# First groups of five sub-layers: hi products of six k first, squares on VectorE, statistics one piece later

## The chip, the cores and the metric

The kernel runs on one core of one Trainium2 chip. The metric is the device time of one launch in microseconds. TensorE is called PE here, VectorE DVE, ScalarE ACT, GpSimd POOL, SyncE SP.

## The reference

One step of a hybrid streaming encoder with two layers, in float32, for a prompt of 16 + 256 frames and a running stream of 32. Each layer has three sub-layers, each wrapped in two RMS norms:

```python
def rmsnorm(x, g):
    x32 = x.astype(jnp.float32)
    y = x32 * lax.rsqrt(jnp.mean(x32 * x32, axis=-1, keepdims=True) + EPS)
    return y.astype(x.dtype) * g

def half_ffn(x, g_pre, w_in, w_out, g_post):
    gate, up = jnp.split(rmsnorm(x, g_pre) @ w_in, 2, axis=-1)
    return x + 0.5 * rmsnorm((jax.nn.silu(gate) * up) @ w_out, g_post)
...
    for l in range(DEPTH):
        xp = half_ffn(xp, norm_ffn1_pre[l], ffn1_w_in[l], ffn1_w_out[l], norm_ffn1_post[l])
        ...
        mp, k_p, v_p, s_p = mixer_prompt(rmsnorm(xp, norm_mix_pre[l]), w_in[l], attn_sinks[l], key_valid)
        xp = xp + rmsnorm(mp @ w_out[l], norm_mix_post[l])
        ...
        xp = half_ffn(xp, norm_ffn2_pre[l], ffn2_w_in[l], ffn2_w_out[l], norm_ffn2_post[l])
```

The model width is 1024, the inner width of an FFN 2816. The mixer projects to 2816 columns, runs sliding-window attention and retention on them, and projects back.

## The kernel before, in words

**Layout.** Features lie on the 128 partitions, the 304 tokens (16 + 256 + 32) on the free axis. `x` is eight blocks (k = 0 to 7) of 128 x 304. The last FFN works on 288 tokens.

**Products.** An f32 product is made of three fp32r matmuls (`mm3`): weight hi by activation hi (L257), weight lo by activation hi (L258), weight hi by activation lo (L260). A *piece* is a 128 x 512 block of weights as hi and lo. `group4` fills four PSUM banks from eight pieces, one per k, so 12 matmuls per piece and 96 per group; its last two pieces (`tail`) go bank by bank. `group2` is the mixer's form with two banks and four pieces.

**Weights.** SP loads raw weights (four buffers ahead), ACT copies a piece to hi (L205), DVE subtracts to lo (L208). `advance` issues splits while buffers allow and while their number is under `st["cap"]`; it is called from `tick`, which a virtual clock drives. `tick` also runs the entries of the list `later` that are due. So the order of every engine's instructions is fixed when the program is written. For the first group of a sub-layer 8 (FFN 1 and mixer) or 4 (second FFN) pieces have buffers of their own (`xhi`, `xlo`).

**A seam.** Five sub-layers follow another one: 1 the mixer of layer 0, 2 its second FFN, 3 the first FFN of layer 1, 4 its mixer, 5 its second FFN. At a seam `pre_norm` makes the eight hi activations (`act_hi`, ACT) and lo activations (`act_lo`, DVE) from `x`, which the last sub-layer's result has to be added to (`step`, DVE, after POOL's multiplications by `s`, L546), and the sum of the squares of `x` (`stat_sq`: ACT squares, POOL or DVE adds). The factor 1/rms of a token is left out of the products and multiplied in behind them. `stats` makes it: a matmul with ones sums `acc` over the partitions (L483, f32, two passes), then DVE, ACT (a root) and DVE (`reciprocal`) give `rb`. In an FFN `pair(0, 0)` and `pair(0, 1)` then take the four banks of the first group to `hh` and `hl` (DVE `tg`, ACT `sg`, DVE `tu`, ACT `hh`, DVE `hl`); in the mixer `done_kv` and `done_q` take them.

**The first group of a seam, before.** `lead=2`: the hi products (L257, L258) of k = 0 and 1 go first, 16 matmuls, then their lo products (L260, 8 matmuls), then k = 2 and on with all three. `act_lo(k)` stands on DVE between the steps of `x`. Of the seven additions of squares four are on POOL (k up to `KA`), three on DVE. `stats` stands in the middle of the tail, its matmul in a bank of its own; its end lifts `st["cap"]`, which until then allows 11 pieces from the sub-layer's start. `hl` lies in memory that the mixer's `kr`, `qr` and other tiles had used, so at seams 2 and 5 its first writer waits for the mixer's last work on them (`state_out`: ACT copies `kr`, L835, POOL multiplies, L838 to L841, SP moves four pieces, POOL adds, L845).

Of the kernel before, what the change touches and what calls it, by code (L numbers as in the profile page):

```python
# [11 lines left out]
ACTF = mybir.ActivationFunctionType  # L12
# [4 lines left out]
DM = 1024  # L17
# [25 lines left out]
HOLD = 12  # L43
X2 = 1000
TAILF = 4
CAP0 = 14
SQ0 = 500
SQD = 500
PREP = 800
KA = 6  # L50
START = (11000, 11713)
D_UNIT = 4100
D_NORM = 2800
# [12 lines left out]
UNSCALE = 1500  # L66
EXTRA = (8, 4)
RAWS = 4


def shape_tables():
# [35 lines left out]
def tile_hybrid_step(ctx, tc, I, O):  # L107
# [9 lines left out]
    def bank():  # L117
        return ps.tile([P, 512], F32, tag="bk", name="bk")
# [320 lines left out]
    def pre_norm(pre, prev):  # L439

        ua = acts(2 * KD)
        acc = small("acc")
        rb = small("rb")
        if prev:
            lo0 = prev.first(ua)
            for k in range(1, KD + 1):
                if k < KD:
                    prev.step(k)
                    act_hi(k, ua, pre)
                if k == 1:  # L450
                    lo0()
                if k > 2:
                    act_lo(k - 1, ua, pre)
                if k < 2:
                    act_lo(k, ua, pre)
                if k > 1:
                    stat_sq(k - 1, acc, 1, DVE if k > KA else POOL)
            prev.residual0()
            stat_sq(0, acc, 1, DVE)
        else:  # L460
            for k in range(4):
                act_hi(k, ua, pre)
                split_one()
                act_lo(k, ua, pre)

            def rest():
                x_in(1)
                start.close()

            def prep(k):  # L470
                act_hi(k, ua, pre)
                act_lo(k, ua, pre)
            later.append((X2, rest))
            for k in range(4, KD):
                later.append((X2 + PREP * (k - 3), lambda k=k: prep(k)))
            for k in range(KD):
                later.append((X2 + SQ0 + SQD * k, lambda k=k: stat_sq(k, acc, 0)))
            later.sort(key=lambda e: e[0])
        st["cap"] = st["use"] + (11 if prev else CAP0)

        def stats():
            b = bank()
            PE.matmul(out=b[:, T0:N], lhsT=ones, rhs=acc[:, T0:], start=True, stop=True)  # L483
            sd = small("sd")
            if prev is None:
                ACT.activation(out=sd[:, T0:], in_=b[:, T0:N], func=ACTF.Sqrt, scale=1.0 / DM, bias=epst)
            else:
                DVE.scalar_tensor_tensor(out=sd[:, T0:], in0=b[:, T0:N], scalar=1.0 / DM, in1=prev.se[:, T0:], op0=ALU.mult,
                                         op1=ALU.add)
                ACT.activation(out=sd[:, T0:], in_=sd[:, T0:], func=ACTF.Sqrt)  # L490
            DVE.reciprocal(out=rb[:, T0:], in_=sd[:, T0:])
            st["cap"] = 1 << 30

        return (lambda k: ua[k][:, T0:]), (lambda k: ua[KD + k][:, T0:]), rb, stats
# [4 lines left out]
    class Post:  # L499
# [41 lines left out]
        def first(self, ua):  # L541
            t, y = self.xg[:, T0:], self.bk[0][:, :N - T0]
            gg = gprod[:, 2 * (self.post[0] // 2) + self.post[1]:][:, 0:1]
            DVE.tensor_tensor(out=t, in0=self.sp, in1=t, op=ALU.mult)
            for j in range(1, KD):
                POOL.tensor_tensor(out=x[:, j, T0:], in0=x[:, j, T0:], in1=self.s[:, T0:], op=ALU.mult)  # L546
            DVE.scalar_tensor_tensor(out=ua[0][:, T0:], in0=y, scalar=gg, in1=t, op0=ALU.mult, op1=ALU.add)

            def lo():
                DVE.scalar_tensor_tensor(out=t, in0=y, scalar=gg, in1=t, op0=ALU.mult, op1=ALU.add)  # L550
                DVE.tensor_tensor(out=ua[KD][:, T0:], in0=t, in1=ua[0][:, T0:].bitcast(F32), op=ALU.subtract)
            return lo

        def residual0(self):
            DVE.tensor_tensor(out=x[:, 0, T0:], in0=x[:, 0, T0:], in1=self.s[:, T0:], op=ALU.mult)
# [24 lines left out]
    def ffn(pre, post, nxt, prev, after=None):  # L580
# [5 lines left out]
        with tc.tile_pool(name="ffn", bufs=1, reuse_waits="tile") as fp, ExitStack() as late:  # L586
# [14 lines left out]
            def done(g):  # L601
                def f(m, bk):
                    if g and m >= 2:
                        pair(g, m - 2, bk)
                    if g == 0 and m == 1 and prev:
                        stats()
                return f

            for g in range(KF // 2):
                if g == 1:  # L610
# [3 lines left out]
                        fin.start(late.enter_context(tc.tile_pool(name="late", bufs=1, reuse_waits="tile")))  # L614
                    if not prev:
                        stats()
                    for j in range(2):
                        pair(0, j, bk)
                if g == 2 and prev and last:
                    prev.inverse()  # L620
                    prev.unscale()
# [3 lines left out]
                    late_gains()  # L625
                if last and 4 <= g < 10:
                    fin.x_in(*divmod(g - 4, 2))
                bk = group4(KD, xh, xl, n, (0, 2, 1, 3), done(g), lead=2 if prev and g == 0 else 1)
            if prev and not last:
                later.append((clock[0] + UNSCALE, prev.inverse))  # L630
                later.append((clock[0] + 2 * UNSCALE, prev.unscale))
# [104 lines left out]
    def mixer(l, prev):  # L736
# [418 lines left out]
                    DVE.tensor_tensor(out=ml[2 + p][:, T0:], in0=zo[p - 2][1], in1=mh[2 + p][:, T0:].bitcast(F32),  # L1155
                                      op=ALU.subtract)

        first = group4(KD, xh, xl, N, (2, 3, 0, 1), lambda m, bk: stats() if m == 0 else None, lead=2)
        close_extra()
        done_kv(0, first[2:])  # L1160
        done_kv(1, first[2:])
        ACT.preload_act_table(ACTF.Exp)
        advance(2)
        for m in range(2):
            done_q(0)(m, first)
        rot_tables()
        xq = [lambda k, f=f: f(k)[:, t0:] for f in (xh, xl)]
        group2(*xq, N - t0, done_q(1))
        for i in range(2):
# [63 lines left out]
```

## Time and profile before

| what | value |
|---|---|
| median of 3 runs | 1207.5 us (1207.25 to 1207.78) |
| profiled execution | 1207.33 us, of which span 1205.5 us |
| mean granted clock of PE | 0.996 |
| PE busy | 1179.0 us, 98% of the span, 8716 instructions |
| DVE, ACT, POOL busy | 833.0, 592.2, 187.1 us |
| first matmul of seams 1 to 5 at | 237.84, 378.67, 606.35, 833.13, 970.19 us |

Busy time is the time in which an engine executes instructions of the profile. PE is the engine that is nearly always busy, so what counts at a seam is how long PE takes from its first matmul to a later one, beside the number of matmuls between. The granted clock is the share of full speed at which the throttle let PE run.

### The profile page before, as it was taken

To read this page: it belongs to the slowest core of one execution; us is meant where nothing else is said; L and a number is where in the kernel's file an instruction comes from. 1 tells how busy PE (TensorE), PEld (TensorE's weight loads), DVE (VectorE), ACT (ScalarE), POOL (GpSimd) and SP (SyncE) were. 2 spreads that over 40 slices of the span, in tenths; PEclk is the share of its full clock that TensorE was granted. 3 is DMA by queue.
4 is the path that set the end of the run, shared out by engine and by line. 5 is a ranking of instruction groups with operands and counts; after the bars stand their busy time and mean duration, and the time that the engine had idled before them with its cause. 6 is when DMAs were issued, how large, how long until landed. Compare 5 with 4: busy or idle time off the path is not lost. (4 is left out here: it accounts for less than half of the span.)

```text
span 1205.5 us, 22774 instructions
## 1 busy us (share of the span) xinstructions
PE 1179.0 (98%) x8716; PEld 1146.9 (95%) x8716; DVE 833.0 (69%) x1497; ACT 592.2 (49%) x1211; POOL 187.1 (16%) x199
## 2 busy tenths in 40 slices
PE   9999999999999999999999999999999999999995
PEld 8999999998899999999989999999988999999995
DVE  7766664587888766675586665747778888766543
ACT  6644444455455545444454444445554655554442
POOL 4200001130143200022030000313101353000000
PEclk9999999999999999999999999999999999999998
DMA  7655455633425554555616445556434436655531
GB/s 229 173 169 178 142 177 159 205 121 109 125 73 156 160 173 141 166 164 159 207 57 192 141 149 177 175 161 199 127 91 133 123 97 199 195 151 179 179 105 40
DMA packets 155309, 182.51 MB, mean 151 GB/s; under 512 B 12016, under 2 KB 125984, under 8 KB 154944
## 3 DMA queue, kind: packets, MB, share of 16 engines
q1 hardware_dynamic: 153488, 178.84, 48.4%
q0 software_dynamic: 1344, 1.76, 0.7%
q8 instruction: 68, 1.11, 0.4%
q10 hardware_dynamic: 368, 0.47, 0.1%
q14 instruction: 41, 0.34, 0.1%
HBM read 175.70 MB, written 2.23 MB: 148 GB/s over the span
## 5 line engine op out<-in xcount | busy, mean ns | idle before, releaser
L257 PE MATMUL bk<-act,hi 128*128 128x304 f32 (+1 forms) x1696 | 515.4, 306 | 1.3 <-ACT hi L205 1.0
L208 DVE TENSOR_TENSOR lo<-raw,hi 128x512 fp32r<-128x512 f32 x616 | 420.9, 729 | 127.2 <-ACT hi L205 123.8
L258 PE MATMUL bk<-act,lo 128*128 128x304 f32 (+1 forms) x1696 | 505.4, 300 | 0.7 <-DVE lo L208 0.7
L260 PE MATMUL bk<-act,hi 128*128 128x304 f32 (+1 forms) x1696 | 489.8, 301 | 2.6 <-DVE act L427 1.2
L205 ACT ACTIVATE hi<-raw 128x512 fp32r<-128x512 f32 x615 | 351.3, 622 | 138.0 <-PE bk L260 111.0
L257 PEld LDWEIGHTS bk<-act,hi 128*128 128x128 f32 x1696 | 319.1, 188 | 7.4 <-issue 3.2
L258 PEld LDWEIGHTS bk<-act,lo 128*128 128x128 f32 x1696 | 319.1, 188 | 2.0 <-DVE lo L208 1.3
L260 PEld LDWEIGHTS bk<-act,hi 128*128 128x128 f32 x1696 | 312.8, 188 | 4.2 <-DVE act L1155 2.4
L257 PE MATMUL bk<-hh,hi 128*128 128x304 f32 (+1 forms) x704 | 210.7, 300 | 0.0
L258 PE MATMUL bk<-hh,lo 128*128 128x304 f32 (+1 forms) x704 | 210.2, 299 | 0.0
L260 PE MATMUL bk<-hl,hi 128*128 128x304 f32 (+1 forms) x704 | 207.8, 301 | 0.0
L595 ACT ACTIVATE sg<-tg 128x304 f32<-128x304 f32 (+1 forms) x88 | 40.0, 455 | 196.5 <-DVE tg L594 196.5
L257 PEld LDWEIGHTS bk<-hh,hi 128*128 128x128 f32 x704 | 132.5, 188 | 0.0
L258 PEld LDWEIGHTS bk<-hh,lo 128*128 128x128 f32 x704 | 132.3, 188 | 0.0
L260 PEld LDWEIGHTS bk<-hl,hi 128*128 128x128 f32 x704 | 131.0, 188 | 0.0
L594 DVE TENSOR_TENSOR tg<-bk,rb 128x304 f32<-128x304 f32 (+1 forms) x88 | 41.0, 466 | 85.9 <-PE bk L260 85.8
L574 POOL TENSOR_TENSOR x<-x,rs 128x304 f32<-128x304 f32 (+1 forms) x40 | 45.4, 1168 | 291.5 <-DVE rs L570 291.5
L599 DVE TENSOR_TENSOR hl<-tu,hh 128x304 fp32r<-128x304 f32 (+1 forms) x88 | 41.5, 472 | 47.6 <-ACT hh L598 45.0
L598 ACT ACTIVATE hh<-tu 128x304 fp32r<-128x304 f32 (+1 forms) x88 | 40.0, 455 | 59.4 <-DVE tu L597 59.4
L513 POOL TENSOR_TENSOR acc<-acc,sq 128x304 f32<-128x304 f32 (+1 forms) x12 | 10.1, 838 | 322.1 <-ACT sq L510 321.5
L546 POOL TENSOR_TENSOR x<-x,s 128x304 f32<-128x304 f32 (+1 forms) x35 | 31.3, 931 | 141.7 <-ACT s L538 141.7
L597 DVE TENSOR_TENSOR tu<-tu,sg 128x304 f32<-128x304 f32 (+1 forms) x88 | 41.8, 475 | 14.2 <-ACT sg L595 9.6
(240 smaller groups left out, 1077.8 us busy)
## 6 DMA issues: line engine op xcount, KB each, us to landing
raw<-in_ffn_w_in_dram SPq DMA_DIRECT2D x352, 256.0 KB, 4.7
raw<-in_ffn_w_out_dram SPq DMA_DIRECT2D x88, 512.0 KB, 4.6
raw<-in_w_in_dram SPq DMA_DIRECT2D x36, 512.0 KB, 4.2
raw<-in_w_out_dram SPq DMA_DIRECT2D x16, 512.0 KB, 3.9
raw<-in_w_in_dram SPq DMA_DIRECT2D x16, 256.0 KB, 3.0
dec<-in_dec_dram SPq DMA_DIRECT2D x2, 1280.0 KB, 7.0
t<-t SPq DMA_DIRECT2D x24, 76.0 KB, 2.1
out_dram<-xgm SPq DMA_DIRECT2D x2, 384.0 KB, 3.6
```

The lines of the kernel that those rows point to most:

```text
L205: ACT.activation(out=hi, in_=r, func=ACTF.Copy)
L208: DVE.tensor_tensor(out=lo, in0=r, in1=hi.bitcast(F32), op=ALU.subtract)
L257: PE.matmul(out=out, lhsT=a, rhs=xh, start=first, stop=False)
L258: PE.matmul(out=out, lhsT=b, rhs=xh, start=False, stop=False)
L260: PE.matmul(out=out, lhsT=a, rhs=xl, start=False, stop=last)
L546: POOL.tensor_tensor(out=x[:, j, T0:], in0=x[:, j, T0:], in1=self.s[:, T0:], op=ALU.mult)
L574: POOL.tensor_tensor(out=x[:, k, T0:], in0=x[:, k, T0:], in1=self.rs[:, T0:], op=ALU.mult)
L594: DVE.tensor_tensor(out=tg[:, T0:], in0=bk[j][:, :n], in1=rb[:, T0:], op=ALU.mult)
L595: ACT.activation(out=sg[:, T0:], in_=tg[:, T0:], func=ACTF.Silu)
L597: DVE.tensor_tensor(out=tu[:, T0:], in0=tu[:, T0:], in1=sg[:, T0:], op=ALU.mult)
L598: ACT.activation(out=hh[a][:, T0:], in_=tu[:, T0:], func=ACTF.Copy)
L599: DVE.tensor_tensor(out=hl[a][:, T0:], in0=tu[:, T0:], in1=hh[a][:, T0:].bitcast(F32), op=ALU.subtract)
```

## The change

In the first group of each of the five seams the hi products of k = 0 to 5 come first (`LEAD = 6`, 48 matmuls), then their lo products (24), then k = 6 and 7. All `act_lo` stand on DVE behind all steps of `x`, and all seven additions of squares stand behind those, on DVE. `first` gives the two instructions of the lo activation of k = 0 apart, behind steps 2 and 3. `stats` runs behind the first piece of the second group (in the mixer behind the first half of one), as an entry of `later`, with what uses `rb` in the same entry; its matmul is two of half the tokens, into free columns of the first group's own banks 0 and 1. The cap on splits is 13 pieces where it was 11. The mixer's `advance(2)` between `done_kv` and `done_q` is gone. The first sub-layer of the program, which follows none, is as it was.

```diff
@@ -43,11 +43,11 @@
 HOLD = 12
 X2 = 1000
 TAILF = 4
+CAP = 13
 CAP0 = 14
 SQ0 = 500
 SQD = 500
 PREP = 800
-KA = 6
 START = (11000, 11713)
 D_UNIT = 4100
 D_NORM = 2800
@@ -66,6 +66,8 @@
 UNSCALE = 1500
 EXTRA = (8, 4)
 RAWS = 4
+LEAD = 6
+STATS = 1500
 
 
 def shape_tables():
@@ -442,19 +444,16 @@
         acc = small("acc")
         rb = small("rb")
         if prev:
-            lo0 = prev.first(ua)
-            for k in range(1, KD + 1):
-                if k < KD:
-                    prev.step(k)
-                    act_hi(k, ua, pre)
-                if k == 1:
-                    lo0()
-                if k > 2:
-                    act_lo(k - 1, ua, pre)
-                if k < 2:
-                    act_lo(k, ua, pre)
-                if k > 1:
-                    stat_sq(k - 1, acc, 1, DVE if k > KA else POOL)
+            low = prev.first(ua)
+            for k in range(1, KD):
+                prev.step(k)
+                act_hi(k, ua, pre)
+                if k in (2, 3):
+                    low[k - 2]()
+            for k in range(1, KD):
+                act_lo(k, ua, pre)
+            for k in range(1, KD):
+                stat_sq(k, acc, 1, DVE)
             prev.residual0()
             stat_sq(0, acc, 1, DVE)
         else:
@@ -476,17 +475,21 @@
             for k in range(KD):
                 later.append((X2 + SQ0 + SQD * k, lambda k=k: stat_sq(k, acc, 0)))
             later.sort(key=lambda e: e[0])
-        st["cap"] = st["use"] + (11 if prev else CAP0)
-
-        def stats():
-            b = bank()
-            PE.matmul(out=b[:, T0:N], lhsT=ones, rhs=acc[:, T0:], start=True, stop=True)
+        st["cap"] = st["use"] + (CAP if prev else CAP0)
+
+        def stats(bk=None):
+
             sd = small("sd")
             if prev is None:
+                b = bank()
+                PE.matmul(out=b[:, T0:N], lhsT=ones, rhs=acc[:, T0:], start=True, stop=True)
                 ACT.activation(out=sd[:, T0:], in_=b[:, T0:N], func=ACTF.Sqrt, scale=1.0 / DM, bias=epst)
             else:
-                DVE.scalar_tensor_tensor(out=sd[:, T0:], in0=b[:, T0:N], scalar=1.0 / DM, in1=prev.se[:, T0:], op0=ALU.mult,
-                                         op1=ALU.add)
+                hw = (N - T0) // 2
+                for i in range(2):
+                    c, b = slice(T0 + i * hw, T0 + (i + 1) * hw), bk[i][:, N:N + hw]
+                    PE.matmul(out=b, lhsT=ones, rhs=acc[:, c], start=True, stop=True)
+                    DVE.scalar_tensor_tensor(out=sd[:, c], in0=b, scalar=1.0 / DM, in1=prev.se[:, c], op0=ALU.mult, op1=ALU.add)
                 ACT.activation(out=sd[:, T0:], in_=sd[:, T0:], func=ACTF.Sqrt)
             DVE.reciprocal(out=rb[:, T0:], in_=sd[:, T0:])
             st["cap"] = 1 << 30
@@ -546,10 +549,12 @@
                 POOL.tensor_tensor(out=x[:, j, T0:], in0=x[:, j, T0:], in1=self.s[:, T0:], op=ALU.mult)
             DVE.scalar_tensor_tensor(out=ua[0][:, T0:], in0=y, scalar=gg, in1=t, op0=ALU.mult, op1=ALU.add)
 
+            def full():
+                DVE.scalar_tensor_tensor(out=t, in0=y, scalar=gg, in1=t, op0=ALU.mult, op1=ALU.add)
+
             def lo():
-                DVE.scalar_tensor_tensor(out=t, in0=y, scalar=gg, in1=t, op0=ALU.mult, op1=ALU.add)
                 DVE.tensor_tensor(out=ua[KD][:, T0:], in0=t, in1=ua[0][:, T0:].bitcast(F32), op=ALU.subtract)
-            return lo
+            return full, lo
 
         def residual0(self):
             DVE.tensor_tensor(out=x[:, 0, T0:], in0=x[:, 0, T0:], in1=self.s[:, T0:], op=ALU.mult)
@@ -602,8 +607,6 @@
                 def f(m, bk):
                     if g and m >= 2:
                         pair(g, m - 2, bk)
-                    if g == 0 and m == 1 and prev:
-                        stats()
                 return f
 
             for g in range(KF // 2):
@@ -614,8 +617,15 @@
                         fin.start(late.enter_context(tc.tile_pool(name="late", bufs=1, reuse_waits="tile")))
                     if not prev:
                         stats()
-                    for j in range(2):
-                        pair(0, j, bk)
+                        for j in range(2):
+                            pair(0, j, bk)
+                    else:
+                        def begin(bk=bk):
+                            stats(bk)
+                            for j in range(2):
+                                pair(0, j, bk)
+                        later.append((clock[0] + STATS, begin))
+                        later.sort(key=lambda e: e[0])
                 if g == 2 and prev and last:
                     prev.inverse()
                     prev.unscale()
@@ -625,7 +635,7 @@
                     late_gains()
                 if last and 4 <= g < 10:
                     fin.x_in(*divmod(g - 4, 2))
-                bk = group4(KD, xh, xl, n, (0, 2, 1, 3), done(g), lead=2 if prev and g == 0 else 1)
+                bk = group4(KD, xh, xl, n, (0, 2, 1, 3), done(g), lead=LEAD if prev and g == 0 else 1)
             if prev and not last:
                 later.append((clock[0] + UNSCALE, prev.inverse))
                 later.append((clock[0] + 2 * UNSCALE, prev.unscale))
@@ -1155,15 +1165,19 @@
                     DVE.tensor_tensor(out=ml[2 + p][:, T0:], in0=zo[p - 2][1], in1=mh[2 + p][:, T0:].bitcast(F32),
                                       op=ALU.subtract)
 
-        first = group4(KD, xh, xl, N, (2, 3, 0, 1), lambda m, bk: stats() if m == 0 else None, lead=2)
+        first = group4(KD, xh, xl, N, (2, 3, 0, 1), lambda m, bk: None, lead=LEAD)
         close_extra()
-        done_kv(0, first[2:])
-        done_kv(1, first[2:])
-        ACT.preload_act_table(ACTF.Exp)
-        advance(2)
-        for m in range(2):
-            done_q(0)(m, first)
-        rot_tables()
+
+        def begin():
+            stats(first)
+            done_kv(0, first[2:])
+            done_kv(1, first[2:])
+            ACT.preload_act_table(ACTF.Exp)
+            for m in range(2):
+                done_q(0)(m, first)
+            rot_tables()
+        later.append((clock[0] + STATS / 2, begin))
+        later.sort(key=lambda e: e[0])
         xq = [lambda k, f=f: f(k)[:, t0:] for f in (xh, xl)]
         group2(*xq, N - t0, done_q(1))
         for i in range(2):
```

PE at seam 2, in the first group; `act_4724` to `act_4731` are the hi activations of before, `act_4732` on the lo ones, `bk_4869` to `bk_4872` the four banks. Before, from the last hi product of k = 1:

```order
L257 MATMUL bk_4872<-act_4725,xhi5_4532 128x304
L258 MATMUL bk_4872<-act_4725,xlo5_4533 128x304
L260 MATMUL bk_4869<-act_4732,xhi4_4528 128x304
L260 MATMUL bk_4870<-act_4732,xhi4_4528 128x304
L260 MATMUL bk_4871<-act_4732,xhi4_4528 128x304
L260 MATMUL bk_4872<-act_4732,xhi4_4528 128x304
L260 MATMUL bk_4869<-act_4733,xhi5_4532 128x304
L260 MATMUL bk_4870<-act_4733,xhi5_4532 128x304
L260 MATMUL bk_4871<-act_4733,xhi5_4532 128x304
L260 MATMUL bk_4872<-act_4733,xhi5_4532 128x304
L257 MATMUL bk_4869<-act_4726,xhi6_4552 128x304
L258 MATMUL bk_4869<-act_4726,xlo6_4553 128x304
```

In the changed kernel the names are one higher (hi `act_4725` on, lo `act_4733` on, banks `bk_4870` on); from the last hi product of k = 5:

```order
L259 MATMUL bk_4873<-act_4730,hi_4581 128x304
L260 MATMUL bk_4873<-act_4730,lo_4582 128x304
L262 MATMUL bk_4870<-act_4733,xhi4_4529 128x304
L262 MATMUL bk_4871<-act_4733,xhi4_4529 128x304
L262 MATMUL bk_4872<-act_4733,xhi4_4529 128x304
L262 MATMUL bk_4873<-act_4733,xhi4_4529 128x304
L262 MATMUL bk_4870<-act_4734,xhi5_4533 128x304
L262 MATMUL bk_4871<-act_4734,xhi5_4533 128x304
L262 MATMUL bk_4872<-act_4734,xhi5_4533 128x304
L262 MATMUL bk_4873<-act_4734,xhi5_4533 128x304
```

The lo products of k = 0 stood behind 16 hi products and stand behind 48.

PE at seam 2, around the statistics matmul (L483 before, L491 now), here without the numbers of the names. Before, in the tail of the first group:

```order
L257 MATMUL bk<-act,hi 128x304
L258 MATMUL bk<-act,lo 128x304
L260 MATMUL bk<-act,hi 128x304
L483 MATMUL bk<-acc,ones 128x304
L257 MATMUL bk<-act,hi 128x304
L258 MATMUL bk<-act,lo 128x304
L260 MATMUL bk<-act,hi 128x304
L257 MATMUL bk<-act,hi 128x304
L258 MATMUL bk<-act,lo 128x304
```

Now, behind the first piece of the second group, whose four lo products are one row:

```order
L259 MATMUL bk<-act,hi 128x304
L260 MATMUL bk<-act,lo 128x304
L259 MATMUL bk<-act,hi 128x304
L260 MATMUL bk<-act,lo 128x304
L262 MATMUL bk<-act,hi 128x304 x4
L491 MATMUL bk<-acc,ones 128x152 x2
L259 MATMUL bk<-act,hi 128x304
L260 MATMUL bk<-act,lo 128x304
L262 MATMUL bk<-act,hi 128x304
```

It moved from inside the tail to the place behind the second group's first piece, and became two of 152 columns.

ACT at seam 2, from the mixer's copy `kr` to the splits of the second group; `sd` is the root in `stats`, `sg` and `hh` belong to the two pairs. Before:

```order
L432 ACTIVATE sq<-x 128x304 x3
L835 ACTIVATE kr<-bk 128x512
L205 ACTIVATE hi<-raw 128x512
L490 ACTIVATE sd<-sd 128x304
L205 ACTIVATE hi<-raw 128x512 x4
L595 ACT_TABLE_LOAD
L595 ACTIVATE sg_4821<-tg_4819 128x304
L598 ACTIVATE hh_4825<-tu_4823 128x304
L595 ACTIVATE sg_4822<-tg_4820 128x304
L598 ACTIVATE hh_4826<-tu_4824 128x304
L205 ACTIVATE hi<-raw 128x512 x7
```

Now:

```order
L434 ACTIVATE sq<-x 128x304 x7
L845 ACTIVATE kr<-bk 128x512
L207 ACTIVATE hi<-raw 128x512 x3
L493 ACTIVATE sd<-sd 128x304
L600 ACT_TABLE_LOAD
L600 ACTIVATE sg_4822<-tg_4820 128x304
L603 ACTIVATE hh_4826<-tu_4824 128x304
L600 ACTIVATE sg_4823<-tg_4821 128x304
L603 ACTIVATE hh_4827<-tu_4825 128x304
L207 ACTIVATE hi<-raw 128x512 x9
```

Before, one split stood ahead of the root and four between it and the first pair; now three stand ahead of the root and none between.

## Rows read from the trace of the kernel before

**Rows 1.** The page, busy time of each engine, its share and instructions.
```profile
PE 1179.0 (98%) x8716; PEld 1146.9 (95%) x8716; DVE 833.0 (69%) x1497; ACT 592.2 (49%) x1211; POOL 187.1 (16%) x199
```

**Rows 2.** PE's waits: PE's group, releaser: idle us, count, longest.
```profile
PE bk L260 <- DVE act L427: 2.5, 7, 0.9
```

**Rows 3.** Timeline of PE, seam 1: start, us, instruction, count, wait in front.
```profile
237.84 0.41 PE L257 MATMUL bk<-act,xhi 128*128 128x304 f32 x1 [0.36 <-DVE act L547]
...
251.88 0.30 PE L260 MATMUL bk<-act,xhi 128*128 128x304 f32 x1
252.25 0.78 PE L483 MATMUL bk<-acc,ones 128*128 128x304 f32 x2
...
253.00 0.30 PE L258 MATMUL bk<-act,xlo 128*128 128x304 f32 x1
...
253.70 0.31 PE L257 MATMUL bk<-act,hi 128*128 128x304 f32 x1
```

**Rows 4.** Timeline of DVE, seam 1.
```profile
242.47 1.11 DVE L564 TENSOR_TENSOR x<-x,act 128x304 f32<-128x304 f32 x1
...
249.26 0.53 DVE L427 SCALAR_TENSOR_TENSOR act<-x,gcol,act 128x304 fp32r<-128x304 f32 x1
```

**Rows 5.** Timeline of ACT, seam 1.
```profile
241.21 0.55 ACT L424 ACTIVATE act<-x,gcol 128x304 fp32r<-128x304 f32 x1 [2.29 <-DVE x L561]
```

**Rows 6.** Timeline of POOL, seam 1.
```profile
236.93 6.32 POOL L546 TENSOR_TENSOR x<-x,s 128x304 f32<-128x304 f32 x7 [35.60 <-ACT s L538]
```

**Rows 7.** Timeline of PE, seam 2.
```profile
378.67 0.41 PE L257 MATMUL bk<-act,xhi 128*128 128x304 f32 x1
...
396.28 0.30 PE L257 MATMUL bk<-act,hi 128*128 128x304 f32 x1
...
404.91 0.30 PE L260 MATMUL bk<-act,hi 128*128 128x304 f32 x1
...
406.21 0.41 PE L258 MATMUL bk<-act,lo 128*128 128x304 f32 x1 [0.32 <-DVE lo L208]
...
409.10 0.30 PE L257 MATMUL bk<-act,hi 128*128 128x304 f32 x1
```

**Rows 8.** Timelines of ACT, POOL and DVE, seam 2.
```profile
392.52 0.58 ACT L835 ACTIVATE kr<-bk 128x512 f32<-128x512 f32 x1
...
393.94 1.37 POOL L840 TENSOR_SCALAR qr<-kr,fint 128x256 f32<-128x256 f32 x1
395.29 0.93 POOL L841 TENSOR_SCALAR qr<-kr,fint 128x256 f32<-128x256 f32 x1
...
402.56 0.48 DVE L599 TENSOR_TENSOR hl<-tu,hh 128x304 fp32r<-128x304 f32 x1 [1.25 <-POOL qr L845]
...
404.81 3.74 ACT L205 ACTIVATE hi<-raw 128x512 fp32r<-128x512 f32 x7
```

**Rows 9.** Timeline of PE, seam 5.
```profile
996.96 0.40 PE L258 MATMUL bk<-act,lo 128*128 128x288 f32 x1 [0.33 <-DVE lo L208]
...
999.71 0.30 PE L257 MATMUL bk<-act,hi 128*128 128x288 f32 x1
```

**Rows 10.** Timelines of PE, DVE and ACT, seam 3.
```profile
606.35 0.41 PE L257 MATMUL bk<-act,xhi 128*128 128x304 f32 x1 [0.36 <-DVE act L547]
...
625.68 0.47 DVE L594 TENSOR_TENSOR tg<-bk,rb 128x304 f32<-128x304 f32 x1
...
629.93 3.23 ACT L205 ACTIVATE hi<-raw 128x512 fp32r<-128x512 f32 x6
```

**Rows 11.** Windows: us, PE, PEld, DVE, ACT, POOL busy, PEclk, DMA; PE's timeline.
```profile
1.04 5.49 PE L346 MATMUL bk<-ones 128*128 128x128 f32 x24 [1.04 <-DVE ones L323]
...
1190.63 0.51 PE L686 MATMUL bk<-c_ident,act 128*96 128x128 f32 x3
...
1194.00:1195.00 1.00, 0.00 (x0) 0.00 (x0) 1.00 (x2) 0.97 (x4) 0.47 (x1) 0.98 0.00 0
1195.00:1205.50 10.50, 0.00 (x0) 0.00 (x0) 4.78 (x7) 3.46 (x7) 2.32 (x1) 0.50 0.38 112
```

## The prediction

> **What bounds the kernel now.** First the page's busy times: PE works 1179.0 us of a span of 1205.5 [rows 1], so some 26 us in all can be won where PE waits. Then PE's waits: the largest one inside the groups is L260 (lo products) behind DVE's `act` of L427, 2.5 us in 7 waits, longest 0.9 [rows 2]. These stand at the seams, so I read the seams as timelines, PE first, then the engine that it waits for.
>
> A unit first. From 396.28 to 404.91 in the second group of seam 2 stand 62 products that wait for nothing [rows 7]: 8.63 / 62 = .139 us from one to the next, and 12 of them, a piece, take 1.67.
>
> Seam 1: from the first product, 237.84, to the first of the next group, 253.70, are 15.86 us [rows 3]. The 96 products need 96 x .139 = 13.36. Of the other 2.50 the statistics matmul takes a part: L260 at 251.88, the two passes, L258 at 253.00; the gap between those two is 1.12 where two intervals (L257 is between) would be .28, so .84. The rest, 1.66, is waiting for activations. Their source: POOL's seven multiplications run from 236.93, .90 each [rows 6], DVE's step takes 1.11 beside them instead of .53 for an operation of that size alone [rows 4], and ACT's hi copy follows with .55 [rows 5]. PE reaches the lo products of k = 0 and 1 after only 16 products (2.2 us) and then runs k by k behind that chain.
>
> Seams 2 and 5 hold a second limit, in the second group. ACT copies `kr` at 392.52; POOL works on it (1.37 and .93 for the last two multiplications), SP moves four pieces, POOL adds; at 402.56 the first pair's `hl` starts on DVE, freed by POOL's L845; at 404.81 ACT goes on to the splits behind the pairs [rows 8]; at 406.21 PE takes the first lo product of the piece that was split there, after .32 of waiting [rows 7]. So that piece comes 406.21 - 392.52 = 13.7 us after `kr`. Before, it is piece 15 (counting from 0), the last of the group, and PE just about doesn't feel it.
>
> **The change, part by part.**
>
> *Hi products of six k first, act_lo and additions behind the steps.* PE now has 48 products, 6.7 us, of hi work before it asks for a lo. At seam 1 the hi of k needs x behind POOL at 236.93 + .90k; step 4 from 240.55 by 1.11, the copy .55, so 242.25 against 237.84 + 32 x .139 = 242.29 where PE asks; k = 5: 243.35 against 243.40. Just in time, so 0 to .3 of waiting. The lo of k = 1 is asked for at 245.1; DVE is through its steps at about 244.4 and adds .53 [rows 4]: 244.95, and from there .53 per lo against .56 per k of PE. So of 1.66 some 1.5 go. What DVE takes over, four additions per seam at about .53, stands behind the lo activations; the sum of squares is ready about 14 us after the first product (7 lo, 6 additions, the residual of block 0 and its square behind the steps), PE asks for it at 13.36 + .1 + .83 = 14.3 in the mixer. No cover is left there but no wait either: 0 to .8, I take 0.
>
> *Statistics in halves.* Two matmuls of 152 columns, two passes each, in place of one. Between the same columns (.84) and twice that for twice the passes (1.62, with .78 for the two passes of [rows 3]) I take 1.05, near the first because the columns are the same: +.2.
>
> Seams 1 and 4 (mixer): -1.5 + .2 = -1.3 each, -1.7 to -.6. Fourteen pieces are split before the statistics there (the cap of 13 binds only with the pairs of an FFN), six of the second group, 10 us of work, and the uses of `rb` fit in.
>
> Seam 3 (FFN, no mixer's memory): first product 606.35, the first group ends at 606.35 + .1 + 13.36 = 619.81. Fourteen pieces are split; the statistics start at 621.5 and end at 622.5; DVE, the root and the reciprocal bring `tg` to about 625.5, where it was 625.68; the splits behind the pairs came 4.25 after `tg` (629.93) [rows 10], so at 629.75, and the piece's lo product 1.4 later (404.81 to 406.21 in [rows 7, 8]), at 631.15. PE is through six pieces and the statistics at 619.81 + 10.0 + 1.05 = 630.9. It stalls for about .3: -1.3 + .3 = -1.0, from -1.6 to 0.
>
> Seams 2 and 5 (second FFN behind the mixer). The same gain in the first group. But the statistics' entry now holds the pairs too, and 13 pieces are all that is split before it: the order shows no split on ACT between the root and the first pair, where four stood. Nothing that lets `hl` start early has changed: `kr`'s copy on ACT still stands behind the last square. I put the copy at .4 earlier (the squares end with the group), and DVE's lo splits beside POOL's multiplications, which raise one from .93 to 1.37 [rows 8], at up to .9 later: net +.1, -.4 to +.9. So the piece behind the pairs has its lo product at 406.3 as before, only that it is piece 13 now. PE: first group to 378.67 + .1 + 13.36 = 392.13, piece 8 to 393.80, statistics to 394.85, pieces 9 to 12 to 401.53. Then PE idles some 4 us (its hi product can go a little ahead of the lo one) until 406.3. Behind that lo product come 35 intervals to the next group, where there were 20 (406.21 to 409.10, [rows 7]): 15 x .139 = 2.09, +.1 = +2.2 against before, between 1.7 and 3.0. What was won in the first group is in this already: it only makes the idle time longer. Seam 5, 288 columns: (999.71 - 996.96 - .11) / 20 = .132 [rows 9]; 15 x .132 + .1 = +2.1, 1.6 to 2.9.
>
> *The rest.* Fewer POOL additions (20 rows) free an engine at 16%: nothing. The mixer's `advance(2)` is taken up by the next tick: nothing. SP's queue stays as it was but for one load that goes one place: nothing, since loads run buffers ahead.
>
> Sum: -1.3 - 1.3 - 1.0 + 2.2 + 2.1 = +.7, on the profiled execution's 1207.33: 1208.0. The median is .17 above that execution: **1208.2**. With the bounds partly against each other this forecast's own range is 1206.9 to 1209.5.
>
> **Rivals.**
>
> *The idle time costs PE's clock (slower).* The trace has one place to read: the last matmuls start at 1190.63 and end at 1191.14; from 1194 to 1195 the granted clock is still .98, from 1195 on .50, the lower level of 1.2 GHz [rows 11]. So PE lost its clock after some 3.8 us without work. Two idle stretches of about 4.0 us come up here, at seams 2 and 5, right at that edge. What it costs afterwards: at the program's start 24 small matmuls take 5.49 us with the clock not yet given [rows 11]; a stretch of that length at half rate loses 2.7 at most, I take 2.3. One of the two: 1210.5; both: 1212.8. For it: the lengths; against it: the stretches may come out at 3.6. Chance .30.
> The Trainium skill ("TensorE: Matmul & The Clock Gate", Part 1, "What's actually happening") says that the throttled state is the default and that activity releases it; the end of this trace agrees (.98, then .50), and by that rule a long enough stall at seams 2 and 5 gives the two prices above.
>
> *The memory's wait does not bind (faster).* If `hl` at seams 2 and 5 is free when the pairs reach it, the pair chain alone counts, as at seam 3: with seam 3's distances `tg` 3.0 after 394.85 and the split 4.25 after that, 402.1; two of the pair's operations on DVE beside POOL's additions at 1.11 instead of .53 [rows 4] make it 403.3, the lo product 404.7. That is 1.5 sooner, twice: 1208.2 - 3.0 = 1205.2. For it: POOL has less to do at the seam. Against: none of the POOL work taken away stands in the chain from `kr` to L845, and `kr` itself isn't moved ahead of the squares. Chance .10.
>
> *The first group goes on waiting (the change doesn't do what it says).* All the ready times above are within .1 of PE's need; if the steps beside POOL run later, each of seams 1, 3 and 4 loses .7 of its gain and the idle stretches stay: the hi work has no cover ahead of k = 4 and 5. With .7 at a fourth place, where a late sum of squares pushes the second groups, +2.1 to +2.8: 1210.3 to 1211. Chance .08, mostly above the bound of change.
>
> **How the numbers follow.** Forecast .52, clock .30, free memory .10, waiting group .08. About .2%, 2.4 us, is what a measurement of this kernel can tell from no change: faster is below 1205.1, slower above 1209.9. The forecast lies inside with its whole range; the free memory ends at the edge, and I count .09 of it as faster; clock and nearly all of the last are slower: .37; same: .54. The range is to hold 8 in 10: it begins below the forecast's 1206.9 at 1206.0, a part of the way to the free memory, and ends at 1211.8, which takes in one lost clock and the waiting group and leaves out both clocks lost and most of the free memory.
>
> **What the profile after will show.** Right: at seam 1 no wait for L429's `act` above .3 and 14.3 us or so from the first product to the statistics; between the two groups no statistics row any more but behind the first piece; at seams 2 and 5 one idle stretch of PE of 3.6 to 4.5 us that ends with `hi` or `lo` of piece 13, with `hl` on DVE waiting for POOL ahead of it; the next group starting at about 411 less what seam 1 won. Wrong: those stretches under 2 us (then `hl` was free, or the split stands elsewhere), waits of more than 1 us in the first groups, or a granted clock below .95 in the windows behind the stretches, which decides for the first rival.

## The result and the profile after

The changed kernel takes 1216.88 us (median of 4 runs, 1215.07 to 1217.34) against 1207.42: ratio 1.0073, 95% interval 1.0061 to 1.0085. It is slower by 9.5 us; the prediction was 1208.2 with a range of 1206.0 to 1211.8. The profiled execution has a span of 1214.9 us (before 1205.5) and a mean clock of 0.991 (before 0.996).

The page's busy times first, which answer to [rows 1]: PE's busy time hasn't grown, so the 9.4 us aren't more work but waiting, and, as shown below, stretches at the lower clock.

```profile
PE 1176.8 (97%) x8726; PEld 1149.2 (95%) x8726; DVE 831.7 (68%) x1522; ACT 595.4 (49%) x1211; POOL 167.1 (14%) x179
```

PE's waits, in total us, count and longest, answer to [rows 2]. The first group was small before:

```profile
PE bk L257 <- ACT hi L205: 1.0, 2, 0.7
```

The second was not there at all. The waits for L427 (now L429) were 2.5 in 7 and are 1.3 in 2. Now:

```profile
PE bk L259 <- ACT hi L207: 9.8, 2, 5.3
PE bk L1055 <- ACT pt L1015: 4.1, 2, 2.4
PE bk L262 <- DVE act L429: 1.3, 2, 1.0
```

Where the time went, as the difference of matching starts on PE in the two traces:

| stretch on PE | before | after | difference |
|---|---|---|---|
| seam 1 to seam 2 (mixer of layer 0) | 140.83 | 141.32 | +0.49 |
| seam 2 to its third group | 30.43 | 34.67 | +4.24 |
| seam 3 to its third group | 29.26 | 27.88 | -1.38 |
| seam 4 to seam 5 (mixer of layer 1) | 137.06 | 138.01 | +0.95 |
| seam 5 to its third group | 29.52 | 35.65 | +6.13 |
| all other stretches up to the last group's end | | | -0.86 |

**Seam 1**, timeline of PE (start, us, instruction, count, wait in front), answers to [rows 3]:

```profile
237.97 0.41 PE L259 MATMUL bk<-act,xhi 128*128 128x304 f32 x1 [0.37 <-DVE act L550]
...
244.77 1.42 PE L262 MATMUL bk<-act,xhi 128*128 128x304 f32 x9
...
251.43 0.30 PE L259 MATMUL bk<-act,hi 128*128 128x304 f32 x1
...
252.12 0.30 PE L262 MATMUL bk<-act,hi 128*128 128x304 f32 x1
252.94 0.79 PE L491 MATMUL bk<-acc,ones 128*128 128x152 f32 x4 [0.52 <-DVE acc L436]
253.46 0.40 PE L259 MATMUL bk<-act,hi 128*128 128x304 f32 x1
```

The L262 row shows the first nine of the 24 lo products. The first group's 96 products take 251.43 - 237.97 = 13.46 us; .139 each makes 13.34. Once begun they no longer wait for an activation, as the prediction's first part said. The statistics wait .52 for the sum of squares, where I took 0 out of 0 to .8.

**Seam 2**, timeline of PE, answers to [rows 7]:

```profile
379.29 0.41 PE L259 MATMUL bk<-act,xhi 128*128 128x304 f32 x1
...
393.36 0.30 PE L260 MATMUL bk<-act,lo 128*128 128x304 f32 x1
394.07 0.41 PE L259 MATMUL bk<-act,hi 128*128 128x304 f32 x1 [0.42 <-ACT kr L845]
...
402.08 0.30 PE L262 MATMUL bk<-act,hi 128*128 128x304 f32 x1
406.90 0.41 PE L259 MATMUL bk<-act,hi 128*128 128x304 f32 x1 [4.52 <-ACT hi L207]
407.63 0.62 PE L260 MATMUL bk<-act,lo 128*128 128x304 f32 x1 [0.32 <-DVE lo L210]
408.05 0.46 PE L262 MATMUL bk<-act,hi 128*128 128x304 f32 x1
...
411.04 0.30 PE L259 MATMUL bk<-act,hi 128*128 128x304 f32 x1
...
413.96 0.30 PE L259 MATMUL bk<-act,hi 128*128 128x304 f32 x1
```

Timelines of DVE, ACT and POOL there, answering to [rows 8]:

```profile
394.57 2.28 DVE L210 TENSOR_TENSOR lo<-raw,hi 128x512 fp32r<-128x512 f32 x3 [0.53 <-ACT hi L207]
396.77 0.53 DVE L492 SCALAR_TENSOR_TENSOR sd<-bk,se 128x152 f32<-128x152 f32 x2
...
403.99 0.48 DVE L604 TENSOR_TENSOR hl<-tu,hh 128x304 fp32r<-128x304 f32 x1 [2.60 <-POOL qr L855]
```

```profile
393.44 0.58 ACT L845 ACTIVATE kr<-bk 128x512 f32<-128x512 f32 x1
...
405.88 0.46 ACT L603 ACTIVATE hh<-tu 128x304 fp32r<-128x304 f32 x1 [0.54 <-DVE tu L602]
406.24 3.73 ACT L207 ACTIVATE hi<-raw 128x512 fp32r<-128x512 f32 x7
```

```profile
394.88 1.88 POOL L850 TENSOR_SCALAR qr<-kr,fint 128x256 f32<-128x256 f32 x1
...
402.69 1.26 POOL L855 TENSOR_TENSOR qr<-qr,kr 128x512 f32<-128x512 f32 x1 [3.24 <-DMA kr<-qr]
```

Piece 13 is split behind both pairs, and the first of these waits 2.60 us for POOL. PE stands still for 4.5 us at seam 2. Before that it waits .42 us in the second group for a bank that ACT's copy `kr` still reads (394.07), a wait that the prediction doesn't have. At seam 5 PE stands still for 5.3 us:

```profile
996.15 0.29 PE L262 MATMUL bk<-act,hi 128*128 128x288 f32 x1
1001.76 0.61 PE L259 MATMUL bk<-act,hi 128*128 128x288 f32 x1 [5.32 <-ACT hi L207]
1002.49 0.61 PE L260 MATMUL bk<-act,lo 128*128 128x288 f32 x1
```

And at both stretches the clock goes: at seam 2 some .3 us after PE works again, at seam 5 some .6 us before it does. Windows of the changed kernel (us, busy time of PE, PEld, DVE, ACT and POOL, then the granted clock, DMA share, GB/s):

```profile
406.00:407.00 1.00, 0.10 (x1) 0.10 (x1) 0.59 (x2) 1.00 (x3) 0.00 (x0) 1.00 0.72 168
407.00:408.00 1.00, 0.68 (x2) 0.46 (x3) 1.00 (x2) 1.00 (x3) 0.00 (x0) 0.61 0.01 0
408.00:409.00 1.00, 1.00 (x5) 1.00 (x5) 1.00 (x3) 1.00 (x3) 0.00 (x0) 0.50 0.02 9
...
411.00:412.00 1.00, 1.00 (x9) 1.00 (x8) 0.67 (x2) 0.94 (x2) 0.00 (x0) 1.00 1.03 238
...
1001.00:1002.00 1.00, 0.24 (x1) 0.24 (x1) 0.72 (x2) 1.00 (x3) 0.00 (x0) 0.57 0.76 279
...
1007.00:1008.00 1.00, 1.00 (x6) 1.00 (x6) 0.99 (x3) 0.01 (x1) 0.00 (x0) 0.51 0.86 271
1008.00:1009.00 1.00, 1.00 (x9) 1.00 (x9) 0.70 (x3) 0.45 (x1) 0.00 (x0) 1.00 0.82 286
```

.50 is the lower level, 1.2 GHz; a product then takes .25 at seam 2 (12 products from 408.05) instead of .139. From piece 13's lo product to the third group are 35 intervals: 413.96 - 407.63 = 6.33 where 35 x .139 + .1 = 4.97, so the clock costs 1.4 there, and at seam 5 (1002.49 to 1009.68, 7.19 for 4.72) 2.5.

**The mixers** hold a loss that I hadn't on my list. PE at 280 to 289 us, in the mixer of layer 0:

```profile
280.62 1.19 PE L1041 MATMUL bk<-kd,qa 64*128 64x192 f32 x8
...
282.77 0.66 PE L1073 MATMUL bk<-pT,vpE 80*64 80x128 f32 x8
...
286.38 0.38 PE L1055 MATMUL bk<-c_ident,pt 128*80 128x128 f32 x2
288.49 0.64 PE L1055 MATMUL bk<-c_ident,pt 128*80 128x128 f32 x4 [1.72 <-ACT pt L1015]
```

Transposes of attention weights (L1055) wait 1.72 us for the exponentials (L1015) and 2.40 in layer 1. Scores of a unit (L1041) stand ahead of another's product with the values (L1073) now. Before, they stood behind it (L1063 the values, L1031 the scores, L1045 the transposes):

```profile
280.97 0.71 PE L1063 MATMUL bk<-pT,vpE 80*64 80x128 f32 x8
...
283.17 0.92 PE L1031 MATMUL bk<-kd,qa 64*128 64x192 f32 x8
...
287.49 0.82 PE L1045 MATMUL bk<-c_ident,pt 128*80 128x128 f32 x6
```

### The profile page after: what moved, and what is told of

Its sections match the earlier page's. It is cut to its first block, busy times and chain, and to the rows that moved or that the text cites. A ratio compares the mean times of both kernels' runs of the same rounds, so it can differ in the third digit from the quotient of the medians.

```text
span 1214.9 us, 22809 instructions
## 1 busy us (share of the span) xinstructions
PE 1176.8 (97%) x8726; PEld 1149.2 (95%) x8726; DVE 831.7 (68%) x1522; ACT 595.4 (49%) x1211; POOL 167.1 (14%) x179
## 4 chain that ended last, share of the span: by engine, by line
PE 81%; DVE 9%; ACT 3%; issue 2%; POOL 2%; DMA 1%; SPq 1%; DVEq 0%; ACTq 0%; POOLq 0%
PE bk L259 26%; PE bk L262 25%; PE bk L260 25%; DVE lo L210 2%; DVE act L429 1%; DVE x L569 1%; DVE acc L436 1%; ACT hi L207 1%; ACT pt L1015 1%; PE bk L881 1%; DVE osb L1161 1%; PE bk L1073 1%; POOL x L549 1%; DMA raw<-in_ffn_w_in_dram 0%; POOL qr L850 0%
## 5 line engine op out<-in xcount | busy, mean ns | idle before, releaser
L259 PE MATMUL bk<-act,hi 128*128 128x304 f32 (+1 forms) x1696 | 516.0, 306 | 11.1 <-ACT hi L207 9.8
L262 PE MATMUL bk<-act,hi 128*128 128x304 f32 (+1 forms) x1696 | 488.0, 301 | 2.7 <-DVE act L429 1.3
L262 PEld LDWEIGHTS bk<-act,hi 128*128 128x128 f32 x1696 | 313.6, 189 | 4.3 <-DVE act L1165 2.3
L262 PE MATMUL bk<-hl,hi 128*128 128x304 f32 (+1 forms) x704 | 207.8, 301 | 0.0
L262 PEld LDWEIGHTS bk<-hl,hi 128*128 128x128 f32 x704 | 131.0, 188 | 0.0
```

The source lines that it names most:

```text
L259: PE.matmul(out=out, lhsT=a, rhs=xh, start=first, stop=False)
L262: PE.matmul(out=out, lhsT=a, rhs=xl, start=False, stop=last)
```

## The experiments

Ratios are against the kernel before, with a 95% interval. `...` in a diff marks lines that are left out.

**The mixer's virtual times set back** (`e1_times`). The clock that orders the mixer's attention is read where the first group ends, as before the change; the chip's work stays the same.

```diff
+        c0 = clock[0]
         def begin():
+            now, clock[0] = clock[0], c0
             stats(first)
...
             rot_tables()
+            clock[0] = now
```

> Only the virtual time at which the mixer queues its attention work and rot_tables is set back to that of the first group's end, as before the change; the statistics stay where the change put them. Theory (the two new waits of PE in the mixers, 1.72 and 2.40 us at 288 and 886 us, come from the attention work being queued 775 ns later in virtual time and so meeting the banks in another order): both waits go, no wait of PE above 1 us between the mixer's first group and its end, 1216.9 - 4.0 = about 1212.9. Rival (they come from rb being ready later on the chip): they stay, 1216.9. The idle stretches at the second FFNs stay in both.

1213.39 us, 1.0049 (1.0034 to 1.0064): 3.5 us less than the changed kernel. Both waits are gone, and PE's order is that of before again:

```profile
279.68 0.71 PE L1073 MATMUL bk<-pT,vpE 80*64 80x128 f32 x8
...
281.88 0.92 PE L1041 MATMUL bk<-kd,qa 64*128 64x192 f32 x8
...
286.23 0.82 PE L1055 MATMUL bk<-c_ident,pt 128*80 128x128 f32 x6
```

The statistics stand 14.97 us after the first product of seam 1, as in the changed kernel, so `rb` comes as late and the rival falls. Seam 1 to seam 2 takes 139.66 and seam 4 to seam 5 135.63, 1.2 and 1.4 us less than before: that is the gain of seams 1 and 4 by itself, and the two waits cost 1.7 and 2.4. Of these 4.1 some .8 are lost again at seam 2, where the clock stays at .50 for 6.8 us in this run instead of 3.4.

**Splits between the statistics and the pairs** (`e2_splits`).

```diff
                             stats(bk)
+                            advance(4)
                             for j in range(2):
                                 pair(0, j, bk)
```

> The changed kernel with four splits issued between the statistics and the two pairs, at the FFN seams. Theory (PE idles 4.5 and 5.3 us at seams 2 and 5 since the split of the piece it needs stands on ACT and DVE behind pairs that wait for the mixer's memory, and the idle time then costs the clock): the idle stretches fall under 1 us, the granted clock stays at 1.00, the second group of seams 2 and 5 ends about 1.3 us earlier than before the change, so 1216.9 - 5.5 - 7.4 = about 1204.0. Rival (the four splits delay the root or wait for buffers themselves, so that the idle time only moves one group on): 1214 to 1217.

1206.0 us, 0.9987 (0.9978 to 0.9996). Both idle stretches are gone, and the clock stays at 1.00 at the seams. The stretches of seams 2 and 5 fall from 34.67 to 27.89 and from 35.65 to 26.65. It misses the expected 1204.0 by 2.0: in the last FFN behind seam 5 PE now waits .84 and 1.16 for `hi`, each with a wait for `lo` behind it, and from its third group to PE's last matmul that FFN takes 195.4 us where it took 191.2 before the change. The rival had the idle time move on whole; so much of it comes back, in one of the two places. In the mixer of layer 1 the clock falls, too, behind the wait for the exponentials, 2.42 us in this run, and seam 4 to seam 5 takes 139.35 us, 1.3 more than in the changed kernel, which kept 1.00 there. This profiled execution (1207.36 us) is one of the longer of the ten.

**The mixer's memory freed earlier** (`e3_kr`). `state_out`, with ACT's copy of `kr`, goes ahead of the squares.

```diff
             for k in range(1, KD):
                 act_lo(k, ua, pre)
+            if after:
+                after()
             for k in range(1, KD):
                 stat_sq(k, acc, 1, DVE)
...
-        if after:
-            after()
```

> The changed kernel with state_out (the copy of kr on ACT and POOL's work behind it, which frees the memory of hl) ahead of the squares at seams 2 and 5. Theory (hl waits for that chain, nothing else): hl starts some 4 us earlier, the idle stretches fall to about 1 us and the clock stays at 1.00: about 1205, or up to 1208 if POOL's work now slows the lo activations on DVE beside it (1.11 us instead of .53 each). Rival (the chain from the statistics to the pairs binds as well): idle stretches of 2 to 3.5 us remain, clock 1.00 there, 1208 to 1211.

1214.28 us, 1.0053 (1.0036 to 1.0070): my theory had 1205 to 1208 and is wrong. `hl` no longer waits for POOL, and yet PE stands still for 3.43 and 3.48 us. That is as long as the rival said, but both times the clock falls, which the rival didn't have. It falls behind the mixer's wait in layer 1 (2.16 us), too. DVE of this kernel at seam 2:

```profile
395.78 2.87 DVE L210 TENSOR_TENSOR lo<-raw,hi 128x512 fp32r<-128x512 f32 x3
398.58 0.52 DVE L494 SCALAR_TENSOR_TENSOR sd<-bk,se 128x152 f32<-128x152 f32 x2
...
403.76 0.48 DVE L604 TENSOR_TENSOR hl<-tu,hh 128x304 fp32r<-128x304 f32 x1 [0.58 <-ACT hh L603]
```

Three lo splits stand ahead of `sd`, so the chain from the statistics to the split of piece 13 is itself almost as long as POOL's. The waiting for the memory was the last link of two nearly equal ones: without it 1.1 of 4.5 us go at seam 2 (1.8 of 5.3 at seam 5). Up to the third group nothing of that is left at seam 2 (34.83 us against 34.67 in the changed kernel), because the clock stays down for 6.8 us instead of 3.4. What the experiment before took away is the third thing both have in common, the place of piece 13 behind the pairs.

**Both edits, times and splits** (`e4_both`).

> The changed kernel with both edits, the virtual time of the mixer's attention and the four splits between statistics and pairs. If the two causes are independent and are the whole loss, every seam keeps its gain of 1.0 to 1.5 us: 1207.4 - 6.5 = about 1200.9, with no wait of PE above 1 us at a seam or in a mixer. If the loss at the seams is elsewhere (a slower first group, lost clock without idle time), it stays above 1207.

1201.18 us, 0.9949 (0.9934 to 0.9964), against 1200.9 expected. No wait of PE above 1 us at a seam or in a mixer. The sum: the five seams keep their gains (-1.2, -2.5, -1.9, -1.4 and -2.9 us by the table's stretches), and 3.9 come back in the last FFN (195.1 us from its third group to PE's last matmul against 191.2).

**All three edits** (`e6_all`, the one before with `state_out` early).

> The version with both edits (virtual time, four splits), and state_out ahead of the squares at seams 2 and 5. That version still loses 3.9 us in the last FFN behind seam 5, where PE waits twice for hi and lo (1.17 and 1.48 us, each followed by .7). Theory (SP's queue: four moves kr<-qr wait there for POOL, and the raw loads stand behind them): with POOL's work earlier the loads go earlier, the two waits go, 1201.2 - 3.9 = about 1197.3, or half of that where the load of the final norm's gains is the other half. Rival (the waits come from the burst of splits behind the pairs on ACT): they stay, 1201.

1200.22 us, 0.9944 (0.9929 to 0.9959). Of the two waits in the last FFN the first goes, the second stays with 1.22: half of the theory. From the third group of seam 5 to the end it gains 1.4 on the version with both edits, and it loses .6 at the seams; the medians' difference, 1.0, lies inside the intervals.

**LEAD = 2, all else kept** (`e7_lead2`, one number of the version with both edits).

```diff
-LEAD = 6
+LEAD = 2
```

> The version with both edits, with LEAD = 2 as before the change and everything else of the change kept (lo activations behind the steps). Theory (the six k of hi work are what covers the lo activations): PE asks for the lo of k = 1 2.8 us after its first product and gets it after 7.1, so some 4 us of waiting at each of five seams: about 1218 to 1222. Rival (the gain of the seams comes from DVE's order, the lead does little): under 1 us per seam, 1202 to 1206.

1223.72 us, 1.0136 (1.0121 to 1.0151). One wait at each seam, for lo of k = 1:

```profile
243.99 0.81 PE L262 MATMUL bk<-act,xhi 128*128 128x304 f32 x4 [3.07 <-DVE act L429]
```

PE waits 3.1 to 3.5 us at each of the five seams, and at all five the granted clock falls to .50, in the wait or up to 1.1 us behind it. So the lead is what pays for the lo activations standing behind the steps.

**Six additions of squares on POOL** (`e8_pool`).

```diff
-                stat_sq(k, acc, 1, DVE)
+                stat_sq(k, acc, 1, DVE if k > 6 else POOL)
```

> The version with both edits, with six of the seven additions of squares on POOL. Theory (an operation of DVE on two SBUF operands takes 1.11 us instead of .53 beside POOL's work, so POOL's additions beside the lo activations make PE wait for lo): waits for act of 1 to 3 us per seam, 1206 to 1215. Rival (POOL's additions start earlier than DVE's and bring the sum of squares earlier; the lo activations have room): 1200 to 1202.

1205.44 us, 0.9986 (0.9976 to 0.9996), 4.3 above the version with both edits, and by neither of my two ways: PE doesn't wait for lo, but for the sum, 1.12 at seam 1 and 1.17 at seam 4. The FFN seams lose .6 to .9 each without such a wait. DVE at seam 1:

```profile
243.99 4.38 DVE L429 SCALAR_TENSOR_TENSOR act<-x,gcol,act 128x304 fp32r<-128x304 f32 x7
250.93 0.48 DVE L436 TENSOR_TENSOR acc<-acc,sq 128x304 f32<-128x304 f32 x1 [2.57 <-POOL acc L436]
```

The last addition, and the residual of block 0 behind it on DVE, wait 2.57 us for POOL's chain of five (5.08 us). DVE's lo activations take 4.38 beside it instead of 3.20 in the version with both edits, which the lead covers.

**The new first group with the statistics of before** (`e9_oldstats`): the kernel before with only `pre_norm` and `LEAD` changed.

> The kernel before with the new order of the first group alone (six k of hi products, lo activations and additions behind the steps, additions on DVE); the statistics stay whole, in a bank of their own, in the tail of the first group, with the splits and the virtual times of before. Theory (the sum of squares is ready 14 us after the first product, and the tail asks for it after 12.5, so the new order needs the later place): PE waits 1.5 to 2 us at the statistics of each seam and the gain is gone: 1206 to 1210. Rival (the later place of the statistics is not needed): 1201 to 1202.

1211.41 us, 1.0029 (1.0019 to 1.0040). A wait at each of the five statistics, 9.9 us in all:

```profile
PE bk L481 <- DVE acc L435: 9.9, 5, 2.2
```

1.8 to 2.2 each, as expected; the total is 1.4 above my bound. At seam 4 the clock fell 1.3 us after a wait of 1.85; at the other four, with waits of 1.8 to 2.2, it didn't.

**The norm's gains loaded later** (`e10_gf`) and **the cap at 11** (`e11_cap`).

> The version with all three edits (virtual time, four splits, state_out ahead of the squares), with the load of the final norm's gains (512 KB) moved from the second to the fourth group of the last FFN. Theory (what that version still loses in the last FFN, 2.5 us behind seam 5, is raw weights that come late at a moment where the DMA queues are nearly full): the load's 1.6 us go, 1200.2 - 1.5 = 1198.7. Rival (the pairs of the second group stand on DVE behind lo splits of any weights, so the load's place doesn't matter): 1200.2.

1200.41 us, 0.9941 (0.9929 to 0.9954): not told apart from 1200.22; the wait of 1.21 stays. The load's place isn't it, and what keeps that wait is left open.

```diff
-CAP = 13
+CAP = 11
```

> The version with two edits (virtual time, four splits), with the cap on splits ahead of the statistics at 11 as before the change. Theory (two splits fewer stand between the sum of squares and the root at seams 2, 3 and 5, but piece 15 is then the one behind the pairs there, and PE needs it about 404.7 where it comes at 406): waits of about 1.5 us at seams 2 and 5, 1201.2 + 3 = 1204. Rival (the root comes 1.4 us earlier by the two splits and makes up for it): 1200.5 to 1201.5.

1206.87 us, 0.9995 (0.9986 to 1.0004), 2.9 above my theory: PE waits 1.71 at seam 2 and 3.37 at seam 5, and at both the granted clock falls to .50. Against the version with both edits these two seams lose 11.1 us by the table's stretches, 5.1 of it in the waits and most of the rest by the clock; the last FFN gives 4.2 back. The profiled execution (1208.05 us) is the longest of eleven; by the medians the two pieces more are worth 5.7 us. The 4 us in the last FFN stand only in runs with both the four splits and the cap at 13; the changed kernel, and this one, take 190.8 us for that stretch. Whether they lose nothing there because they arrive later is not shown.

## Why the prediction was wrong

Right were the seams themselves. Seams 1 and 4 were to gain 1.3 each and gain 1.2 and 1.4 once the mixers' waits are taken out (`e1_times`); seam 3 was to gain 1.0 and gains 1.4, with the stall of .3 before the piece behind the pairs. The mechanism at seams 2 and 5 is the one that was written down: piece 13 behind pairs that wait for POOL, PE out of pieces 22.9 us after the seam's first product (22.9 forecast), one idle stretch that ends with `hi` of piece 13. That the 22.9 agree is luck: the statistics took .5 less than the sum had, and the wait for the bank that `kr` is copied from gave .6 back.

The sum said +.7 on PE's chain and it was +9.6. Wrong were three things.

First, the choice between forecast and first rival. I gave the lost clock .30 and left it out of the time; it fell at both stretches and cost 1.4 and 2.5, where the rival had 2.3 each. The idle time was 4.5 and 5.3 instead of 4.0, but the argument with an edge near 3.8 fails as such: in other runs the clock fell with waits of 1.7 to 3.5 as well.

Second, the line on what the mixer's part costs: "nothing". It looked at `advance(2)` alone. The entry in `later` also moves the moment at which the attention work is queued by one tick of 775 ns, and all its due times with it, but not those of the rest of the mixer. That turned the order of scores and value products on PE, and cost 1.7 and 2.4 us. PE's order of instructions in the mixers holds this already; the prediction read the order at the seams only. With both, the rival's 1212.8 for two lost clocks becomes 1216.9. That this is the measured time to the tenth is luck: the third error adds 2.2, and a cheaper clock (-.7), seam 3 (-.4) and the other stretches (-.9) take it back.

Third, the length of the idle stretch. I let `kr` be copied .4 earlier, since the squares would end with the group; it stands at 14.15 us after the start of seam 2, where it stood at 13.85, and .7 later at seam 5. In front of it on ACT stands the square of block 0 in both kernels, and that waits for DVE, which now has all seven additions to do first. One of POOL's multiplications (L850) takes 1.88 beside three lo splits on DVE. (The two that the prediction calls POOL's last, 1.37 and .93, are the second and third of five.) Together the piece comes .8 later at seam 2 and 1.7 at seam 5, where the sum had .1 (the bound was .9). Without the clock the two stretches cost 2.8 and 3.6 more than before, where the sum had 2.2 and 2.1. My rival of the free memory took 1.5 off each, and the run that freed it took 1.1 and 1.8 off the idle time; what it had left out are the three lo splits ahead of `sd`: `tg` comes 5.4 us after the statistics there (396.31 to 401.71), where it had 3.0.

Too dear was the statistics in halves: I took 1.05. At seam 2, where they wait for nothing, they cost .52 by the way in which .84 was read: from the product ahead of them (394.88) to the second one behind (395.68) are .80, less two intervals. The .84 held a part of a wait, though: at seam 1, where both kernels wait first, it is .77 from the statistics' start to the second product behind (252.94 to 253.71) and was .75 (252.25 to 253.00), so the halves change nothing there.

The cause is settled as far as the 9.5 us go: 3.5 vanish with the virtual times alone, 10.9 with the splits alone, 15.7 with both. The single gains sum to 14.4; in each of the two runs the clock cost more elsewhere (.8 at seam 2, 1.3 in a mixer), which goes the same way. The later place of the statistics was not tried by itself, apart from their halves and their new bank.

## What to carry to other kernels

When a step that frees a resource (statistics, which let the outputs be read) moves later, look at what stands behind it in the same queue and count how many finished inputs the bounding engine still has: here two more finished pieces or four splits in between decided over about 6 and 11 us. Where a virtual clock orders the program, a step that is entered later carries its whole list of due times with it, so compare the orders far behind the change and not only at it. Price an idle stretch of TensorE with the clock that may go behind it.

## What the runs showed of the hardware

The granted clock fell also with short stretches without work: 3.1 to 3.5 us (LEAD = 2, five times), 3.4 and 3.5 (the memory freed earlier), 1.7 and 3.4 (the cap at 11), 1.85 (statistics of before, seam 4). Four others of 1.8 to 2.2 (statistics of before) kept 1.00. The same wait in the mixer of layer 1 kept it in the changed kernel (2.40) and lost it in two other runs (2.42 with the splits, 2.16 with the memory freed earlier). Several times it fell while PE was working again, .3 us behind the stretch at seam 2 of the changed kernel, and latest with the cap at 11: there the stretch ends at 405.04, the window from 406 to 407 has 1.00, the next one .51.

```profile
406.00:407.00 1.00, 1.00 (x9) 1.00 (x9) 1.00 (x3) 1.00 (x4) 0.00 (x0) 1.00 0.01 4
407.00:408.00 1.00, 1.00 (x7) 1.00 (x6) 1.00 (x2) 1.00 (x3) 0.00 (x0) 0.51 0.74 177
```

After its fall it stayed at .50 for 3.4 us at seam 2 of the changed kernel and for 6.8 at seam 5. By the Trainium skill ("TensorE: Matmul & The Clock Gate", Part 1, "What's actually happening") the throttled state is the default and activity releases it; these rows agree with that, and they show that the length of a stretch alone doesn't tell here whether the clock goes.
